# The first-layer gates of a two-layer hybrid mixer leave PSUM first, and the work behind its fixed first stage is placed anew

## The chip, the cores and the metric

The kernel runs on one core of one Trainium2 chip. The metric is device time in microseconds (us), the median of several executions; lower is better. A trace of one execution shows the engines: PE (TensorE, matmuls and transposes), DVE (VectorE), ACT (ScalarE), POOL (GpSimd) and SP, which here issues most of the DMAs. Each engine works through its own queue in order.

## What is computed

The reference is a trunk of two layers over 1024 tokens of width 1024. Cut to what matters:

```
for l in range(2):
  shift, scale, gate = split(SiLU(c) @ W_mod[l] + b_mod[l])
  h = RMSNorm(x) * (1 + scale) + shift
  aq,ak,av,ag, rq,rk,rv,rg, gq,gk,gv,gg,ga = split(h @ W_in[l])
  A = sliding_window_attention(rope(aq), rope(ak), av, sinks) * SiLU(ag)
  B = rms(retention(rot(rq), rot(rk), rv)) * SiLU(rg)
  C = rms(gated_linear_attention(gq, gk, gv, log_sigmoid(ga @ gw + gb) / 16)) * SiLU(gg)
  x = x + gate * RMSNorm(concat(A, B, C) @ W_out[l])
```

Everything is float32. The kernel makes each large product from three fp32r products, of high and low parts: hi x hi, lo x hi, hi x lo.

## The kernel before

**Tiles.** The tokens are eight tiles of 128. For each tile, `pre` (line 601) takes the norm: squares on ACT (L598), the sum and its power -0.5 (L582 on DVE, L583 on POOL), the scaling on DVE (L613). After a delay it transposes the tile on PE in two halves of four blocks (L620, printed under the helper's line L180), applies gain and shift (L627 on ACT for the first half, L629 on DVE for the second), and splits the result into its high part (L633, ACT) and low part (L634, DVE). The product of a tile with a weight unit of 256 columns is 24 matmuls (`accum`, printed under the helper's line L165).

**Gates.** Layer 0 begins with the gates, in four rounds of two tiles: unit `gg` (272 columns, with the low-rank logits) for both tiles, then `rg` (256) for both. Before the second half of the first x tiles is ready, `gg` of tiles 0 and 1 run over the first half alone. Each product lies in one of three PSUM banks (tag `mm`) until it has been taken out: for `gg`, L1084 copies the 16 logits and L1076 takes a tanh, both on ACT, and L1078 on DVE forms the SiLU; for `rg`, L1076 and L1078. The logits are transposed later and go through exponential and logarithm (L1106 to L1111). The SiLU values go to DRAM by SP. Behind the gates come `rq`, `rk` and `rv`, which need the sine and cosine tables (DVE L367 to L395, sine on ACT L391 and L392; L402 and four transposes per tile pair turn them round for later).

**What sets the order.** A hand-written first stage (`first`, line 660) issues the first modulation, x tiles 0 and 1, and the units `gg` and `rg`, inside a block in which DVE, ACT, POOL and SP keep the written order; the norms of tiles 2 and 3 are in that block too. PE keeps the written order everywhere. Outside the block a scheduler orders the other four engines ahead of time, by priority (written order, unless a block asks for high priority) among what it takes to be ready and to have a free tile. The written order comes from a planner: a clock `clk` that advances by a cost per PE instruction, and jobs (generators) that resume when the clock passes their due time. The due times are the table `L`. For the first layer's x tiles: `pf2` and `pf3` place the transposes of tiles 2 and 3; tile t of 4 to 7 takes its norm at `pf4 + pf5 * (t - 4)` and its transposes `pre1` = 7.44 later.

**Tiles in SBUF that matter.** `t2` (128x512) has ten buffers: x tiles 4 to 7 take eight (loaded by L639), and the normalised and modulated tiles need the same kind. `t1` has eight, `sm` eleven, and `st`, the staging tiles of weight loads, five. Weights come in four chunks per unit; `whi` (L758 on DVE or L760 on ACT) writes a chunk's high part, `wlo` (L763, POOL) its low part; later units do this in L149, L151 and L486.

**Small work.** POOL clears an accumulator for the gate part of the modulation (L309, whose first load is L310) and two large buffers of the linear attention (L877); these are held behind `mark[0]`, the power (L583) of tile 3. DVE halves `gnc` (L859) and copies the sinks (L888) from `sinkn`, an `sm` tile that SP fills.

Of the kernel before, what the change touches and what calls it, by code (L numbers as in the profile page):

```python
# [93 lines left out]
def trunk(ctx: ExitStack, tc: tile.TileContext, ins, cst, out):  # L94
    nc = tc.nc
    V, A, G, T = nc.vector, nc.scalar, nc.gpsimd, nc.tensor
# [4 lines left out]
    cp = ctx.enter_context(tc.tile_pool(name="const", bufs=1))  # L101
# [20 lines left out]
    def small(w, dt=F32):  # L122
        return gp.tile([P, w], dt, tag="sm", name=nm("sm"), bufs=BS)
# [7 lines left out]
    def f(ap):  # L131
        return ap.bitcast(F32)
# [11 lines left out]
    def eng(k):  # L144
        return G if EN[k] == "G" else V
# [251 lines left out]
    def tables_T():  # L397

        for p in range(NP_):
            yield L["tt1"]  # L400
            rep_ = t2()
            V.tensor_copy(rep_.rearrange("p (s t h k) -> p s t h k", s=2, t=2, h=4),  # L402
                          sincos[:, 2 * p:2 * p + 2, :, 0:32].rearrange("p t s k -> p s t k").unsqueeze(3)
                          .to_broadcast((P, 2, 2, 4, 32)))
            yield L["tt2"]
            pt = aux()
# [7 lines left out]
    gnc = cp.tile([P, DEPTH], F32, name="gnc")  # L414
# [126 lines left out]
    def sw_second():  # L541
        drain()
        for k in range(4):
# [46 lines left out]


    hT = {}
    mark = [None] * 2

    def squares(xt, to):
        ss = small(2)
# [4 lines left out]
    def pre(l, t, xt, soon=None):  # L601

        p, tt = divmod(t, 2)
        if tt == 0:
            hT[(l, p)] = place(TOK[l][p])
        h = hT[(l, p)]
        xn = [t2(), t2()]
        r = rstd2(squares(xt, xn))
        for j in range(2):
            if EN[f"xn{j}"] == "A":  # L610
                A.activation(xn[j], xt[j], AF.Copy, scale=r)
            else:
                V.tensor_scalar(xn[j], xt[j], r, None, ALU.mult)  # L613
        yield L[soon] if soon else lat("pre1", l)
        for j in range(2):
            yield (0.0, ("modh", l, j))
            x = aux()
            for k in range(4):
                kt = 4 * j + k
                transp(x[:, k * P:(k + 1) * P], xn[j][:, k * P:(k + 1) * P], ident)  # L620
            hf = t2()
            for k in range(4):
                kt = 4 * j + k
                ks = slice(k * P, (k + 1) * P)
                gain, shift = modc[(l, 1)][:, kt:kt + 1], modc[(l, 0)][:, kt:kt + 1]
                if EN[f"mod{j}"] == "A":
                    A.activation(hf[:, ks], x[:, ks], AF.Identity, scale=gain, bias=shift)  # L627
# [5 lines left out]
            A.activation(hi, hv, AF.Copy)  # L633
            eng(f"hlo{j}").tensor_tensor(lo, hv, f(hi), ALU.subtract)  # L634
        flag(("hT", l, t), 3.0)

    def load_x(t, xt, eng_):
# [22 lines left out]
    def first(wp):  # L660
# [54 lines left out]
        xn, at, ss, hv = {}, {}, {}, {}  # L715
# [39 lines left out]
        def whi(n, kc, st, e):  # L755
            d = w[n][:, 0, 2 * kc:2 * kc + 2, 0:256]
            if e is V:
                V.tensor_copy(d, st)  # L758
            else:
                A.activation(d, st, AF.Copy)  # L760

        def wlo(n, kc, st):
            G.tensor_tensor(w[n][:, 1, 2 * kc:2 * kc + 2, 0:256], st, f(w[n][:, 0, 2 * kc:2 * kc + 2, 0:256]),  # L763
                            ALU.subtract)
# [3 lines left out]
        sg = ga_load(0)  # L768
# [40 lines left out]
        rst = [next(rgen) for _ in range(4)]  # L809
# [7 lines left out]
        pc = cols_a(1)  # L817
        yield
        w["rg"] = unit(0, "rg")
        for kc in (0, 1):  # L820
            whi("rg", kc, rst[kc], A)
            wlo("rg", kc, rst[kc])
        cols_r(1, pc)
        for t in range(2):
# [34 lines left out]
    V.tensor_scalar(gnc, gnc, 0.5, None, ALU.mult)  # L859
    kv = {}  # L860

    gat = []
# [19 lines left out]
                gz["sc"] = [z_[:, 1024 * j:1024 * j + 1024].rearrange("p (c h q) -> p c h q", c=2, h=4)  # L882
                            for j in range(2)]
    sink8 = cp.tile([P, 2, 8], F32, name="sink8")
    sinkn = small(16)
    nc.sync.dma_start(sinkn, sinks.rearrange("(o a) b -> o (a b)", o=1).to_broadcast((P, 16)))
    for l in range(DEPTH):
        V.tensor_copy(sink8[:, l].rearrange("p (m r) -> p m r", r=2),  # L888
                      sinkn[:, 8 * l:8 * l + 8].rearrange("p (r m) -> p m r", r=2))
# [183 lines left out]
    def silu2(pg):  # L1073

        th = t1()
        A.activation(th, pg, AF.Tanh, scale=0.5)  # L1076
        sg = t1()
        V.scalar_tensor_tensor(sg, th, 1.0, pg, ALU.add, ALU.mult)  # L1078
        return sg


    def gla_logits(l, t, pg, pa):
        ga = small(16)
        A.activation(ga, pa, AF.Copy)  # L1084
# [683 lines left out]
L = {"sw1": 0.4, "ld1": 1.2, "ld2": 1.2, "ld1@1": 1.2, "ld2@1": 1.27, "swW00": 0.0, "swT1": 0.0, "swW11": 0.4, "swW10": 0.5, "tt1": 8.0, "tt2": 1.75, "tb1": 24.5, "tb2": 0.75, "pf2": 7.0, "pf3": 8.5, "pf4": 17.3, "pf5": 4.16, "mod1": 4.6, "mod2": 4.0, "mod3": 13.29, "mod4": 7.04, "mod5": 3.36, "mod6": 9.04, "pre1": 7.44, "kv1": 3.1, "kv2": 2.11, "aq1": 6.0, "aq7": 6.0, "ag1": 5.44, "aq2": 2.4, "aq6": 5.2, "aq3": 10.21, "aq4": 7.36, "aq5": 3.6, "hn1": 8.93, "hn2": 2.85, "gz1": 11.18, "gz2": 8.13, "gl1": 2.76, "gd3": 15.9, "gc1": 0.62, "gc2": 1.94, "gc3": 1.33, "gc4": 0.87, "gc6": 0.86, "gc5": 1.14, "rc1": 0.8, "rc2": 1.09, "rc3": 5.87, "rc4": 2.51, "fin1": 7.28, "lay1": 1.13, "gc4@1": 0.93, "mod2@1": 4.0, "mod3@1": 15.1, "mod5@1": 3.36, "mod6@1": 4.11, "pre1@1": 7.44, "kv1@1": 2.79, "kv2@1": 5.28, "aq1@1": 4.8, "aq7@1": 5.28, "ag1@1": 6.25, "aq2@1": 0.82, "aq6@1": 6.0, "aq3@1": 10.9, "aq4@1": 4.4, "aq5@1": 5.15, "hn1@1": 8.12, "hn2@1": 2.85, "gz1@1": 15.91, "gz2@1": 10.94, "gl1@1": 4.6, "gd3@1": 15.9, "gc1@1": 0.48, "gc2@1": 1.94, "gc3@1": 1.33, "gc6@1": 0.86, "gc5@1": 1.04, "rc1@1": 0.37, "rc2@1": 0.84, "rc3@1": 1.9, "rc4@1": 2.79, "fin1@1": 4.28, "lay1@1": 1.7}  # L1768
# [44 lines left out]
```

## Time and profile before

| what | us |
| --- | --- |
| median of 3 runs | 1010.38 |
| lowest and highest | 1010.09 and 1011.06 |
| the profiled execution | 1010.98 |
| its span, first to last instruction | 1009.3 |
| PE busy | 971.7 (96%) |
| DVE busy | 687.8 (68%) |
| ACT busy | 410.9 (41%) |
| POOL busy | 249.0 (25%) |
| mean granted PE clock | 0.985 |

How to read what follows: in a timeline, a line has its start in us from the span's start, its length, engine, source line (L1076 is line 1076 of the kernel before), operation, output and inputs by tile name, shape, and a count where equal instructions were merged; in brackets stands how long the engine was idle before it and who ended that. In the list of waits stand who waited for whom, the total, how often, and the longest. In a table of stretches stand for each stretch its length, the busy time of PE, PEld (weight loads), DVE, ACT and POOL with counts, then the granted PE clock, the share of the DMA engines and GB/s.

### The profile page before, as it was taken

To read this page: it belongs to the slowest core of one execution; us is meant where nothing else is said; L and a number is where in the kernel's file an instruction comes from. 1 tells how busy PE (TensorE), PEld (TensorE's weight loads), DVE (VectorE), ACT (ScalarE), POOL (GpSimd) and SP (SyncE) were. 2 spreads that over 40 slices of the span, in tenths; PEclk is the share of its full clock that TensorE was granted. 3 is DMA by queue.
4 is the path that set the end of the run, shared out by engine and by line. 5 is a ranking of instruction groups with operands and counts; after the bars stand their busy time and mean duration, and the time that the engine had idled before them with its cause. 6 is when DMAs were issued, how large, how long until landed. Compare 5 with 4: busy or idle time off the path is not lost.

```text
span 1009.3 us, 19637 instructions
## 1 busy us (share of the span) xinstructions
PE 971.7 (96%) x7133; PEld 828.2 (82%) x7133; DVE 687.8 (68%) x1673; ACT 410.9 (41%) x1154; POOL 249.0 (25%) x314
## 2 busy tenths in 40 slices
PE   6879899999999999999999999999999999999996
PEld 2579899988998777777889999997899877777775
DVE  4768856767766687664588285685676578567886
ACT  3457221333332556642356242123333266664331
POOL 2421101232421233430114010113232033544100
PEclk9888999999999999999999999999999999999999
DMA  9740611433325245668646151343132424378884
GB/s 330 274 149 22 194 47 58 144 118 112 116 85 178 82 143 155 207 178 267 210 154 214 48 158 55 96 141 106 43 116 86 125 76 135 112 233 261 266 262 139
DMA packets 112304, 148.76 MB, mean 147 GB/s; under 512 B 12064, under 2 KB 63820, under 8 KB 112208
## 3 DMA queue, kind: packets, MB, share of 16 engines
q1 hardware_dynamic: 106512, 137.96, 43.6%
q10 hardware_dynamic: 5696, 9.56, 2.6%
q8 instruction: 56, 0.92, 0.4%
q14 instruction: 40, 0.33, 0.1%
HBM read 109.20 MB, written 36.18 MB: 144 GB/s over the span
## 4 chain that ended last, share of the span: by engine, by line
PE 75%; DVE 8%; DMA 8%; issue 2%; ACT 2%; POOL 2%; SPq 0%; ACTq 0%; POOLq 0%; DVEq 0%
PE mm L165 57%; PE aux L165 14%; PE aux L180 4%; DMA st<-in_w_in_dram 3%; DVE arena L486 1%; DMA xk<-in_x_dram 1%; POOL sm L583 1%; DMA st<-in_w_last_dram 1%; DMA wm<-in_w_mod_dram 1%; DMA a<-mixS 1%; DVE t L613 0%; DVE st L547 0%; DVE t L1334 0%; DMA st<-in_w_mod_dram 0%; DVE t L1065 0%
## 5 line engine op out<-in xcount | busy, mean ns | idle before, releaser
L165 PE MATMUL mm<-arena,arena 128*128 128x256 f32 (+2 forms) x1824 | 301.6, 319 | 7.1 <-DVE t L1078 4.0
L165 PE MATMUL mm<-arena 128*128 128x256 f32 (+2 forms) x1824 | 300.8, 319 | 1.3 <-DVE t L1078 1.3
L165 PEld LDWEIGHTS mm<-arena,arena 128*128 128x128 f32 x1824 | 255.5, 191 | 32.1 <-issue 7.8
L165 PEld LDWEIGHTS mm<-arena 128*128 128x128 f32 x1824 | 256.2, 192 | 25.5 <-issue 3.3
L583 POOL TENSOR_TENSOR sm<-sm,mhalf 128x1 f32<-128x1 f32 (+1 forms) x64 | 55.4, 866 | 334.6 <-DVE sm L582 312.1
L165 PE MATMUL mm<-arena,mx 128*128 128x512 f32 (+1 forms) x564 | 130.5, 387 | 1.3 <-ACT kept L1427 1.3
L165 PEld LDWEIGHTS mm<-arena,mx 128*128 128x128 f32 x564 | 101.5, 188 | 25.2 <-ACT kept L1427 1.7
L149 ACT ACTIVATE t<-aux 128x256 f32<-128x256 f32 (+2 forms) x124 | 55.7, 467 | 75.1 <-PE aux L180 64.3
L149 ACT ACTIVATE arena<-st 128x512 fp32r<-128x512 f32 x94 | 56.2, 627 | 54.2 <-DMA st<-in_w_in_dram 19.9
L1015 POOL TENSOR_TENSOR smx<-smx,sm 128x512 f32<-128x512 f32 x32 | 35.7, 1116 | 128.2 <-DVE sm L1014 115.5
L486 DVE TENSOR_TENSOR arena<-st,arena 128x512 fp32r<-128x512 f32 x74 | 59.3, 826 | 4.2 <-ACT arena L149 1.5
L1011 ACT ACTIVATE smx<-smx,sm 128x129 f32<-128x129 f32 x128 | 49.9, 392 | 28.9 <-DVE sm L1008 28.8
L317 DVE SCALAR_TENSOR_TENSOR acc<-st,c_act,acc 128x512 f32<-128x512 f32 x60 | 47.5, 791 | 18.5 <-DMA st<-in_w_mod_dram 17.9
L486 POOL TENSOR_TENSOR arena<-st,arena 128x512 fp32r<-128x512 f32 x26 | 36.5, 1406 | 80.4 <-ACT arena L149 73.3
L180 PE MATMUL aux<-c_ident,t 128*128 128x128 f32 (+1 forms) x292 | 47.9, 281 | 5.0 <-DVE t L402 2.7
L180 PEld LDWEIGHTS aux<-c_ident,t 128*128 128x128 f32 (+1 forms) x292 | 34.9, 144 | 12.0 <-DVE t L402 2.9
L165 PEld LDWEIGHTS aux<-t,mx 32*128 32x128 f32 (+1 forms) x896 | 39.5, 187 | 3.9 <-issue 2.2
L1059 ACT ACTIVATE t<-aux 128x256 f32<-128x256 f32 x32 | 12.3, 383 | 73.2 <-PE aux L165 66.4
L165 PE MATMUL aux<-t,mx 32*128 32x32 f32 (+1 forms) x896 | 40.7, 272 | 0.0
L1006 DVE COPY_PREDICATED smx<-c_curmask,aux 128x256 f32<-128x256 int32 x64 | 25.4, 446 | 18.7 <-ACT smx L149 15.2
L627 ACT ACTIVATE t<-aux,mod,mod 128x128 f32<-128x128 f32 x56 | 21.5, 460 | 39.8 <-DVE t L1334 18.9
L1334 DVE SCALAR_TENSOR_TENSOR t<-t,sm,t 128x512 f32<-128x512 f32 x32 | 24.0, 780 | 18.7 <-DMA t<-in_x_dram 11.9
(230 smaller groups left out, 1406.2 us busy)
## 6 DMA issues: line engine op xcount, KB each, us to landing
st<-in_w_in_dram SPq DMA_DIRECT2D x96, 256.0 KB, 3.7
st<-in_w_mod_dram SPq DMA_DIRECT2D x64, 256.0 KB, 3.1
mx<-mixS SPq DMA_DIRECT2D x20, 512.0 KB, 5.5
mixS<-t SPq DMA_DIRECT2D x72, 128.0 KB, 3.4
st<-in_w_last_dram SPq DMA_DIRECT2D x36, 256.0 KB, 4.0
wm<-in_w_mod_dram SPq DMA_DIRECT2D x12, 512.0 KB, 6.8
t<-in_x_dram SPq DMA_DIRECT2D x24, 256.0 KB, 5.3
t<-tabS SPq DMA_DIRECT2D x16, 256.0 KB, 4.4
```

The lines of the kernel that those rows point to most:

```text
L149: A.activation(dst, src, AF.Copy)
L165: T.matmul(dst, lhsT, rhs, start=start, stop=stop)
L180: T.transpose(dst, src, idn)
L317: V.scalar_tensor_tensor(acc, wt, c_act[:, k:k + 1], acc, ALU.mult, ALU.add)
L486: e.tensor_tensor(lo, st, f(hi), ALU.subtract)
L583: mark[1] = G.tensor_tensor(r, r, mhalf[:, :w], ALU.pow)
L627: A.activation(hf[:, ks], x[:, ks], AF.Identity, scale=gain, bias=shift)
L1006: V.copy_predicated(sv, curmask.unsqueeze(1).to_broadcast((P, 2, P)), pv[:, :, n // P - 1, :])
L1011: A.activation(sm[:, h, :], sm[:, h, :], AF.Exp, bias=mx[:, h:h + 1], accum_out=sums[:, h:h + 1])
L1015: eng("pn").tensor_tensor(sm[:, :, 0:128], sm[:, :, 0:128], rs.unsqueeze(2).to_broadcast((P, 4, P)), ALU.mult)
L1059: A.activation(sq, po, AF.Square)
L1334: V.scalar_tensor_tensor(xt[j], yg[j], r, xt[j], ALU.mult, ALU.add)
```

## The change

- `silu2` (tanh and SiLU of both gates) and the copy of the logits are put in blocks of high priority.
- `mark[0]` becomes the power (L583) of tile 7 in place of that of tile 3, so the memsets L309 and L877 are queued on POOL behind it. `mark[2]` follows the latest L634.
- In `first`, all four chunks of `rg` are converted ahead of the second modulation of tiles 0 and 1 (chunk 2 on DVE, the others on ACT); before, chunks 2 and 3 were converted on DVE behind it.
- `pf2` and `pf3` grow by 1.0, `pf4` shrinks by 4.1.
- The halving of `gnc` and the copies of the sinks become a job due 44 us of the planner's time later, queued behind `mark[2]`; `sinkn` gets a buffer of its own.
- SBUF kept back for software DMA is set to 1024 bytes per partition.

```diff
-    mark = [None] * 2
+    mark = [None] * 3
...
                 V.tensor_scalar(xn[j], xt[j], r, None, ALU.mult)
+        if l == 0 and t == NT - 1:
+            mark[0] = mark[1]
         yield L[soon] if soon else lat("pre1", l)
...
-            eng(f"hlo{j}").tensor_tensor(lo, hv, f(hi), ALU.subtract)
+            mark[2] = eng(f"hlo{j}").tensor_tensor(lo, hv, f(hi), ALU.subtract)
...
-        for kc in (0, 1):
-            whi("rg", kc, rst[kc], A)
+        for kc in range(4):
+            whi("rg", kc, rst[kc], V if kc == 2 else A)
             wlo("rg", kc, rst[kc])
         cols_r(1, pc)
...
             flag(("hT", 0, t), 2.6)
-        for kc in (2, 3):
-            whi("rg", kc, rst[kc], V)
-            wlo("rg", kc, rst[kc])
         flag(("w", 0, "rg"), 3.0)
...
         pump()
-    mark[0] = mark[1]
     for t in range(4, NT):
...
-    V.tensor_scalar(gnc, gnc, 0.5, None, ALU.mult)
...
-    sinkn = small(16)
+    sinkn = cp.tile([P, 16], F32, name="sinkn")
     nc.sync.dma_start(sinkn, sinks.rearrange("(o a) b -> o (a b)", o=1).to_broadcast((P, 16)))
-    for l in range(DEPTH):
-        V.tensor_copy(sink8[:, l].rearrange("p (m r) -> p m r", r=2),
-                      sinkn[:, 8 * l:8 * l + 8].rearrange("p (r m) -> p m r", r=2))
+
+    def small_work():
+        yield 44.0
+        with tc.issue_after(mark[2].ins):
+            V.tensor_scalar(gnc, gnc, 0.5, None, ALU.mult)
+            for l in range(DEPTH):
+                V.tensor_copy(sink8[:, l].rearrange("p (m r) -> p m r", r=2),
+                              sinkn[:, 8 * l:8 * l + 8].rearrange("p (r m) -> p m r", r=2))
+
+    job(small_work())
...
         th = t1()
-        A.activation(th, pg, AF.Tanh, scale=0.5)
         sg = t1()
-        V.scalar_tensor_tensor(sg, th, 1.0, pg, ALU.add, ALU.mult)
+        with tc.high_priority():
+            A.activation(th, pg, AF.Tanh, scale=0.5)
+            V.scalar_tensor_tensor(sg, th, 1.0, pg, ALU.add, ALU.mult)
         return sg
...
         ga = small(16)
-        A.activation(ga, pa, AF.Copy)
+        with tc.high_priority():
+            A.activation(ga, pa, AF.Copy)
...
-L = {... "pf2": 7.0, "pf3": 8.5, "pf4": 17.3, "pf5": 4.16, ...}
+L = {... "pf2": 8.0, "pf3": 9.5, "pf4": 13.2, "pf5": 4.16, ...}
...
-    nc = _bacc.Bacc("TRN2", target_bir_lowering=False, num_devices=1)
+    nc = _bacc.Bacc("TRN2", target_bir_lowering=False, num_devices=1, dynamic_dma_scratch_size=1024)
```

More of the change, by code (lines that the diff above doesn't have):

```diff
@@ L1767 @@
 EN = {"shw0": "V", "shw1": "A", "shw2": "A", "shw3": "A", "slw0": "V", "slw1": "G", "slw2": "V", "slw3": "G", "sht2": "A", "sht3": "A", "sht4": "A", "slt2": "V", "slt3": "G", "slt4": "G", "sd": "V", "mh0": "A", "mh1": "A", "mh2": "A", "mh3": "A", "mf": "A", "ms0": "V", "ms1": "V", "ms2": "V", "ms3": "V", "yg0": "V", "yg1": "V", "ml0": "V", "ml1": "V", "ml2": "V", "ml3": "V", "mod0": "A", "mod1": "V", "qst": "S", "smh": "S", "sml": "S", "sm0": "S", "sm1": "S", "lao": "S", "sao": "S", "lmix": "S", "ssg": "S", "lsg": "S", "ssr": "S", "lsr": "S", "lx": "S", "sx": "A", "lw": "S", "lwm": "S", "whi0": "V", "whi1": "A", "whi2": "A", "whi3": "A", "wlo0": "V", "wlo1": "V", "wlo2": "V", "wlo3": "G", "xn0": "V", "xn1": "V", "hlo0": "V", "hlo1": "V", "rot0": "V", "rot1": "V", "rdec": "V", "kslo": "V", "qslo": "V", "vlo": "G", "kT": "A", "qT": "A", "sprev": "A", "pn": "G", "pf0": "A", "aoc": "A", "hng": "V", "mh": "A", "gso": "V", "mg": "V", "mgl": "V", "rT": "A", "rv": "A", "gv": "A", "gk": "A", "ak0": "V", "ak1": "V", "ak2": "V", "ak3": "V", "kd0": "G", "kd1": "G", "kd2": "G", "kx1": "G", "kx2": "G", "kx3": "V", "kx4": "V", "qb": "G", "stx": "V"}
-L = {"sw1": 0.4, "ld1": 1.2, "ld2": 1.2, "ld1@1": 1.2, "ld2@1": 1.27, "swW00": 0.0, "swT1": 0.0, "swW11": 0.4, "swW10": 0.5, "tt1": 8.0, "tt2": 1.75, "tb1": 24.5, "tb2": 0.75, "pf2": 7.0, "pf3": 8.5, "pf4": 17.3, "pf5": 4.16, "mod1": 4.6, "mod2": 4.0, "mod3": 13.29, "mod4": 7.04, "mod5": 3.36, "mod6": 9.04, "pre1": 7.44, "kv1": 3.1, "kv2": 2.11, "aq1": 6.0, "aq7": 6.0, "ag1": 5.44, "aq2": 2.4, "aq6": 5.2, "aq3": 10.21, "aq4": 7.36, "aq5": 3.6, "hn1": 8.93, "hn2": 2.85, "gz1": 11.18, "gz2": 8.13, "gl1": 2.76, "gd3": 15.9, "gc1": 0.62, "gc2": 1.94, "gc3": 1.33, "gc4": 0.87, "gc6": 0.86, "gc5": 1.14, "rc1": 0.8, "rc2": 1.09, "rc3": 5.87, "rc4": 2.51, "fin1": 7.28, "lay1": 1.13, "gc4@1": 0.93, "mod2@1": 4.0, "mod3@1": 15.1, "mod5@1": 3.36, "mod6@1": 4.11, "pre1@1": 7.44, "kv1@1": 2.79, "kv2@1": 5.28, "aq1@1": 4.8, "aq7@1": 5.28, "ag1@1": 6.25, "aq2@1": 0.82, "aq6@1": 6.0, "aq3@1": 10.9, "aq4@1": 4.4, "aq5@1": 5.15, "hn1@1": 8.12, "hn2@1": 2.85, "gz1@1": 15.91, "gz2@1": 10.94, "gl1@1": 4.6, "gd3@1": 15.9, "gc1@1": 0.48, "gc2@1": 1.94, "gc3@1": 1.33, "gc6@1": 0.86, "gc5@1": 1.04, "rc1@1": 0.37, "rc2@1": 0.84, "rc3@1": 1.9, "rc4@1": 2.79, "fin1@1": 4.28, "lay1@1": 1.7}
@@ new lines @@
+L = {"sw1": 0.4, "ld1": 1.2, "ld2": 1.2, "ld1@1": 1.2, "ld2@1": 1.27, "swW00": 0.0, "swT1": 0.0, "swW11": 0.4, "swW10": 0.5, "tt1": 8.0, "tt2": 1.75, "tb1": 24.5, "tb2": 0.75, "pf2": 8.0, "pf3": 9.5, "pf4": 13.2, "pf5": 4.16, "mod1": 4.6, "mod2": 4.0, "mod3": 13.29, "mod4": 7.04, "mod5": 3.36, "mod6": 9.04, "pre1": 7.44, "kv1": 3.1, "kv2": 2.11, "aq1": 6.0, "aq7": 6.0, "ag1": 5.44, "aq2": 2.4, "aq6": 5.2, "aq3": 10.21, "aq4": 7.36, "aq5": 3.6, "hn1": 8.93, "hn2": 2.85, "gz1": 11.18, "gz2": 8.13, "gl1": 2.76, "gd3": 15.9, "gc1": 0.62, "gc2": 1.94, "gc3": 1.33, "gc4": 0.87, "gc6": 0.86, "gc5": 1.14, "rc1": 0.8, "rc2": 1.09, "rc3": 5.87, "rc4": 2.51, "fin1": 7.28, "lay1": 1.13, "gc4@1": 0.93, "mod2@1": 4.0, "mod3@1": 15.1, "mod5@1": 3.36, "mod6@1": 4.11, "pre1@1": 7.44, "kv1@1": 2.79, "kv2@1": 5.28, "aq1@1": 4.8, "aq7@1": 5.28, "ag1@1": 6.25, "aq2@1": 0.82, "aq6@1": 6.0, "aq3@1": 10.9, "aq4@1": 4.4, "aq5@1": 5.15, "hn1@1": 8.12, "hn2@1": 2.85, "gz1@1": 15.91, "gz2@1": 10.94, "gl1@1": 4.6, "gd3@1": 15.9, "gc1@1": 0.48, "gc2@1": 1.94, "gc3@1": 1.33, "gc6@1": 0.86, "gc5@1": 1.04, "rc1@1": 0.37, "rc2@1": 0.84, "rc3@1": 1.9, "rc4@1": 2.79, "fin1@1": 4.28, "lay1@1": 1.7}
```

## The prediction

> **What bounds the kernel now.** I read the page first, then the waits of the matmul engine (PE), then the timeline of its first 130 us.
>
> ```profile
> span 1009.3 us, 19637 instructions
> PE   6879899999999999999999999999999999999996
> ```
> ```profile
> PE mm L165 <- DVE t L1078: 5.3, 2, 4.0
> PE mm L165 <- ACT arena L633: 3.2, 2, 2.2
> PE aux L180 <- DVE t L402: 2.7, 1, 2.7
> PE aux L180 <- DVE t L613: 1.8, 1, 1.8
> ```
>
> A digit is a tenth of a slice of 25 us. From the sixth slice to the last but one PE is at 9, so from about 125 us on its own work is the time; only the first five slices have room. The second view (total wait, times, longest) names the holes there: PE waits for the gate evacuation (L1078), for the normalised x tiles (L633, L613) and for the rotary tables (L402). Whatever closes such a hole ahead of 125 us should arrive at the end nearly in full, since PE runs back to back behind it. The span is 1009.3 us; the profiled execution took 1010.98, so 1.7 us lie around the span. My sum is made against 1010.98; the median of the three runs, 1010.38, is 0.6 below it.
>
> **First hole, 45 to 58 us.** PE's timeline there, then the other engines':
>
> ```profile
> 42.62 2.65 PE L165 MATMUL mm<-arena,arena 128*128 128x256 f32 x21
> 47.98 1.11 PE L180 MATMUL aux<-c_ident,t 128*128 128x128 f32 x8 [1.83 <-DVE t L613]
> 53.42 4.61 PE L165 MATMUL mm<-arena,arena 128*128 128x256 f32 x24 [3.97 <-DVE t L1078]
> 99.72 3.13 PE L165 MATMUL mm<-arena 128*128 128x256 f32 x24 [1.32 <-DVE t L1078]
> ```
> ```profile
> 48.69 1.50 ACT L627 ACTIVATE t<-aux,mod,mod 128x128 f32<-128x128 f32 x4 [6.98 <-PE aux L180]
> 52.31 0.18 ACT L1084 ACTIVATE sm<-mm 128x16 f32<-128x16 f32 x1
> 52.37 0.39 ACT L1076 ACTIVATE t<-mm 128x256 f32<-128x256 f32 x1
> ```
>
> The `mm` pool has three banks. The `gg` gates of tiles 0 and 1 and the `rg` gate of tile 0 fill them; the `rg` gate of tile 1 (53.42) needs the first bank back. Its product was complete before 42.62, when PE went on to `rg`. But ACT stands idle for 6.98 us with L627 of x tile 2 at its head and comes to L1084 and L1076 at 52.3, with DVE's L1078 behind them. As far as the trace shows, only their place in ACT's queue keeps them back: 3.97 us.
>
> The price goes on after the hole:
>
> ```profile
> 53.40:57.80 4.40, 4.38 (x24) 4.40 (x25) 3.52 (x12) 1.72 (x5) 1.57 (x3) 0.61 0.21 69
> 99.70:106.00 6.30, 6.28 (x52) 6.28 (x53) 6.19 (x15) 3.67 (x9) 2.43 (x5) 1.00 0.51 149
> ```
>
> In this table of stretches (length, then PE, PEld, DVE, ACT, POOL busy, granted clock) the 24 products behind the hole run at a clock of 0.61 and take 4.61 us; the same 24 at 99.72, at 1.00, take 3.13. So 1.5 us more belong to it. The Trainium skill, "TensorE: Matmul & The Clock Gate", part 1 on the clock gate, says that an idle window of about 3.4 us halves the clock until PE has been busy for as long. The trace agrees (0.61 behind 3.97 us); by that rule alone one half-clock window costs about 1.7 us, an estimate from the page.
>
> **Second hole, 70 to 81 us.**
>
> ```profile
> 61.10 0.18 ACT L1084 ACTIVATE sm<-mm 128x16 f32<-128x16 f32 x1 [2.58 <-PE mm L165]
> 61.44 0.64 ACT L598 ACTIVATE t<-t 128x512 f32<-128x512 f32 x1
> 63.82 0.88 DVE L613 TENSOR_SCALAR t<-t,sm 128x512 f32<-128x512 f32 x2 [0.66 <-POOL sm L583]
> 69.83 1.05 PE L180 MATMUL aux<-c_ident,t 128*128 128x128 f32 x8
> 73.20 0.76 PE L165 MATMUL mm<-arena,arena 128*128 128x272 f32 x4 [2.21 <-ACT arena L633]
> 77.55 3.81 PE L165 MATMUL mm<-arena,arena 128*128 128x272 f32 x17
> ```
>
> Tile 4 is transposed only when all gates of tiles 0 to 3 are through (69.83), and its modulation and split (L627 to L634) then lie bare: the 3.2 us of the waits, 2.21 of them at 73.20. The 17 products at 77.55 take 224 ns each, against 130 ns at 99.72: 1.6 us. Together 4.8.
>
> **The change part by part.**
>
> *Gates at high priority (L1076, L1078, L1084).* No operation is added. Banks come free at about 43 to 46 us, each evacuation taking 0.18 + 0.39 us of ACT. The 3.97 goes, and with it the 1.5 of slow clock: 5.5. In layer 1 the same priority gains nothing, since PE's digits are 9 there, in the middle of the span.
>
> *Memsets behind the norm of tile 7.* Rows of now:
>
> ```profile
> 43.59 0.88 DVE L613 TENSOR_SCALAR t<-mx,sm 128x512 f32<-128x512 f32 x2 [1.58 <-POOL sm L583]
> 45.47 2.85 DVE L613 TENSOR_SCALAR t<-mx,sm 128x512 f32<-128x512 f32 x2 [0.74 <-POOL sm L583]
> 45.84 1.80 POOL L877 MEMSET mx<- 128x2048 f32 x1
> 81.69 0.99 POOL L583 TENSOR_TENSOR sm<-sm,mhalf 128x1 f32<-128x1 f32 x1 [4.54 <-DVE sm L582]
> ```
>
> The same two L613 take 0.88 us alone and 2.85 beside the memset. Moved away, tile 3 is normalised 2.0 us earlier and the 1.83 before its transposes goes. The memsets (this one, its twin and the smaller one of `acc`) turn up past tile 7's norm, now at 81.69, where DVE is fuller. They cost it between 0 and the 2.0 us seen here; I charge the 2.0 below. SP's load of `acc` (L310) is queued behind the `acc` memset, and stores and weight loads behind that; nothing that PE needs at once, so 0, with 3 us as the far end, the length of the second hole.
>
> *The second half of `rg`'s conversion brought forward.*
>
> ```profile
> 33.11 1.13 ACT L760 ACTIVATE arena<-st 128x512 fp32r<-128x512 f32 x2
> 35.15 0.16 DVE L710 TENSOR_TENSOR sm<-mm,sm 128x4 f32<-128x4 f32 x1 [2.13 <-PE mm L165]
> 39.90 0.75 DVE L758 CAST arena<-st 128x512 fp32r<-128x512 f32 x2
> 40.40 2.65 POOL L763 TENSOR_TENSOR arena<-st,arena 128x512 fp32r<-128x512 f32 x2 [4.09 <-DVE arena L758]
> 36.44 0.81 ACT L743 ACTIVATE t<-aux,mod,mod 128x128 f32<-128x128 f32 x2 [2.20 <-DVE mod L712]
> ```
>
> One conversion more on ACT (0.57) ends at about 34.8, inside the 2.20 that ACT idles before 36.44; one on DVE (0.4) falls into the 2.13 that DVE waits for PE before L710. POOL then runs its two subtractions (2.65) right behind the first two instead of at 40.4 to 43, beside the modulation of tiles 0 and 1; taken as 0, and 1.9 at worst, what the memset cost L613. For that POOL is free at once for tile 2's L583, which stood behind them until 43.05.
>
> *Transposes (pf2 to pf5 and tile order).* Tiles 2 and 3 go 1 us later in PE's order: behind `rg` of tile 0, and seven products into `rg` of tile 1, which can now run. That is 0 where L613 is early. Tiles 4 to 7 go 4.1 us of the planner's time earlier, tile 4 into `rg` of tile 3, so that about 17 products (2.2 us) and the end of the first hole cover its modulation: of the 4.8 I count all, with 1.6 (clock alone) as the lower end. Their norms need free `t2` tiles (ten, of which the x loads take eight) from tiles 2 and 3, and these come some 2 to 3 us earlier.
>
> *Small work.*
>
> ```profile
> 53.84 0.16 DVE L859 TENSOR_SCALAR gnc<-gnc 128x2 f32<-128x2 f32 x1
> 54.23 0.23 DVE L888 COPY sink<-sm 128x8 f32<-128x8 f32 x2
> ```
>
> These leave the middle of tile 3's modulation and run later: some 0.4 us of DVE, moved and not saved. `sinkn` no longer takes one of eleven `sm` tiles. The DMA scratch setting moves addresses only; no software queue appears on the page (q1 and q10 are hardware). 0 for these.
>
> **What is late next: DVE.**
>
> ```profile
> 64.00:118.00 54.00, 46.81 (x363) 45.76 (x361) 45.17 (x111) 33.16 (x81) 8.99 (x16) 0.94 0.35 112
> 82.00:94.00 12.00, 12.00 (x101) 11.94 (x100) 10.92 (x26) 7.82 (x18) 1.64 (x5) 1.00 0.06 22
> 94.00:100.00 6.00, 4.68 (x37) 4.43 (x37) 4.33 (x10) 5.94 (x11) 0.43 (x2) 1.00 0.08 25
> 106.00:118.00 12.00, 9.31 (x81) 9.10 (x79) 10.57 (x30) 3.67 (x9) 1.36 (x1) 1.00 0.69 219
> 130.00:500.00 370.00, 368.12 (x2803) 312.73 (x2803) 248.10 (x625) 141.62 (x424) 92.16 (x113) 1.00 0.45 140
> ```
>
> The third busy number is DVE. The stall sum is 5.5 + 1.8 + 4.8 = 12.1 us. But from 64 to 118 us DVE has 45.2 us of work, 47.2 with the memsets' 2.0, and PE's last hole there (2.7 us, L402) is DVE's backlog. The stage up to 64 ends 7 us sooner (5.5 + 1.8, less 0.3 for tile 2's split), at 57. At the densest long stretch of now, 10.92 of 12 or 0.91, 47.2 us take 51.9 and end at 108.9: 9.1 us gained. At 0.88 (106 to 118) they take 53.6 and end at 110.6: 7.4. Some of that work (L317 for `modg`) can slip past 118 us. I take **8.5 us**: 1010.98 - 8.5 = 1002.5, and 0.6 lower for a median, **1002**.
>
> One more queue matters, ACT's function tables:
>
> ```profile
> 95.06 1.28 ACT L391 ACT_TABLE_LOAD   x1
> 96.35 0.64 ACT L391 ACTIVATE sincos<-t 128x512 f32<-128x512 f32 x1
> 99.24 0.42 DVE L1078 SCALAR_TENSOR_TENSOR t<-t,mm 128x256 f32<-128x256 f32 x1 [1.47 <-ACT t L1076]
> ```
>
> A gate's tanh put between logarithm and sine at high priority adds one load of 1.28 us, where ACT is nearly full (5.94 of 6 at 94 to 100). The 1.32 us before 99.72 therefore stays in my sum. The Trainium skill, "ScalarE: Activation LUTs", on what a table load costs, speaks against the change here: it adds 1.38 us of drain to each switch. The trace disagrees: the L391 load starts at 95.06 and its first sine at 96.35, 1.29 later. By the page one added switch would take about 2.7 us from the 8.5, an estimate.
>
> **The rivals.**
>
> *DVE takes it back.* The first hole goes, the second or the table stage keeps the rest: 3 to 7 us, 1004 to 1008, say 1005. For it: DVE at 0.88 before 118, the L402 wait. Against: from 130 us on DVE is busy 248.1 of 370 us, so a backlog drains there.
>
> *The gates still leave late.* L1084 and L1076 may be held by what they write (`sm`, `t1` tiles) and not by order. Then only the 1.8 for tile 3 and little else goes: 1009, or no change.
>
> *ACT blocks on gates (slower).* Place: ACT's queue, 57 to 90 us. A queue that meets a gate before PE has finished it waits, with the squares (L598) of the next x tile behind it; at 61.10 that costs 2.58 us today, ahead of L598. High priority can put every gate so. Price: 2.6 for each of tiles 4 to 7, 10.3 us on tiles that PE then awaits, against 5.5 gained early: about 5 slower, 1015. It decides as soon as such a wait exceeds the lead of the tile's transposes: by today's rows less 7 us, tile 4's squares come near 54.4 (61.44), its norm ends near 57.7 (63.82 + 0.88), and its transposes stand near 60.6 (69.83, and 2.2 for the 17 products), a lead of about 3. Against it: today's wait of 2.58 is under that lead.
>
> **How the numbers follow.** Forecast, 6.5 to 13.5 gained (997 to 1004): 0.55. DVE takes it back (1004 to 1008): 0.20. Gates late (1008 to 1011): 0.08, of which 0.05 is still faster. ACT blocks (1012 to 1018): 0.14. Better than all that (under 997; the L402 hole goes too): 0.03. The range 997 to 1010 holds the first three but for a sliver, 0.81. A measurement tells about 0.2% from no change: faster 0.55 + 0.20 + 0.05 + 0.03 = 0.83, same 0.03, slower 0.14.
>
> **What would show it.** Right: no PE wait on L1078 near 50 us, L1076 of the first gates before the first L627; L613 of tile 3 near 0.9 for two; clock 1.0 at 48 to 60; tile 4's transposes between products of `rg` tile 3; memsets L877 past the last L583 of the x tiles; the 24 products now at 99.72 (`rg` of tile 6) 8 to 12 us earlier, and the end 7 to 10. Wrong: ACT waits on PE at L1084 with L598 behind and PE waits on L633; a longer wait on L402; one more table load before the sine.

## The result, and the profile after

The changed kernel took 1006.28 us (median of 8 runs) against 1011.77 us for the kernel before: a ratio of 0.9935, 95% interval 0.9914 to 0.9956. One of the eight executions took 3279.62 us; the ratio leaves it out. A second series (`changed_again` below) gave 1003.52 against 1011.28, 0.9914 [0.9885, 0.9943]. The change is faster by 0.4 to 1.2%; by medians the gain is 5.5 and 7.8 us, against the 8.5 of the forecast. The forecast of 1002 lies 4.3 and 1.5 us below the two medians. Both lie in its range of 997 to 1010, but only the second lies in the 997 to 1004 of the forecast itself; 1006.28 lies in the 1004 to 1008 of the rival "DVE takes it back". The profiled execution took 1006.7 us, with a span of 1005.0.

The page of the changed kernel, span and PE's busy tenths (slices of 25 us), then its list of PE's waits (total, times, longest). In it the lines stand a little lower: L1090, L1082 and L1083 are the L1084, L1076 and L1078 of before, L635 is L633, L765 is L763, L753 is L751:

```profile
span 1005.0 us, 19647 instructions
PE   6989799999999999999999999999999999999896
```
```profile
PE aux L180 <- DVE posr L358: 6.0, 1, 6.0
PE aux L180 <- DVE t L402: 5.3, 1, 5.3
PE mm L165 <- DMA wm<-in_w_mod_dram: 3.7, 6, 1.3
PE mm L165 <- ACT arena L635: 3.4, 5, 1.6
```

The third digit went from 7 to 9, the fifth (100 to 125 us) from 8 to 7. The wait on the gates has gone from the list and the one on L402 has doubled, from 2.7 to 5.3. Then PE's timeline at the places that the prediction named:

```profile
45.65 3.00 PE L165 MATMUL mm<-arena,arena 128*128 128x256 f32 x24
...
49.28 1.07 PE L165 MATMUL mm<-arena,arena 128*128 128x256 f32 x7
...
50.98 2.25 PE L165 MATMUL mm<-arena,arena 128*128 128x256 f32 x17
...
54.29 3.31 PE L165 MATMUL mm<-arena 128*128 128x272 f32 x24 [0.47 <-ACT arena L635]
58.35 0.64 PE L165 MATMUL mm<-arena 128*128 128x272 f32 x3 [0.76 <-ACT arena L635]
...
70.36 1.16 PE L165 MATMUL mm<-arena,arena 128*128 128x272 f32 x7 [1.57 <-ACT arena L635]
...
71.39 2.37 PE L165 MATMUL mm<-arena,arena 128*128 128x272 f32 x17
...
92.17 5.92 PE L165 MATMUL mm<-arena 128*128 128x256 f32 x48
...
107.96 1.11 PE L180 MATMUL aux<-c_ident,t 128*128 128x128 f32 x4 [5.26 <-DVE t L402]
```

The wait on L402 in the kernel before was another one, for the second of these copies; the first came without a wait:

```profile
117.57 0.66 PE L180 MATMUL aux<-c_ident,t 128*128 128x128 f32 x4 [2.69 <-DVE t L402]
```

And the table of stretches, changed kernel (length, PE, PEld, DVE, ACT, POOL busy, clock):

```profile
47.00:61.00 14.00, 12.77 (x103) 12.27 (x103) 6.83 (x17) 8.19 (x22) 1.88 (x3) 1.00 0.29 85
61.00:109.00 48.00, 40.38 (x324) 39.20 (x324) 43.67 (x107) 33.90 (x79) 17.32 (x22) 0.99 0.40 125
```

Where the time came from is read off three pairs of rows. The `rg` products begin at 45.65 us; before, at 42.62. So this execution was 3.03 us behind at a place ahead of which, of the whole change, only the earlier conversion of `rg` could act. Most of that is no effect of the change: `changed_again`, the same kernel, is there at 43.42 (more on this in the last section). The products of `rg` of tile 6 begin at 92.17 against 99.72: 7.55 ahead, so 10.58 gained between the two places (10.66 in `changed_again`, 43.42 to 89.86). Then L402's wait gives back time: 5.26 against 2.69 before. That leaves 10.58 - 2.57 = 8.0. The spans differ by 4.3, or 7.3 with the 3.03 added, so 0.7 more is lost further back; I did not trace it.

### The profile page after: what moved, and what is told of

It is laid out like the page before. It is cut to its first block, busy times and chain, and to the rows that moved or that the text cites. A ratio compares the mean times of both kernels' runs of the same rounds, so it can differ in the third digit from the quotient of the medians.

```text
span 1005.0 us, 19647 instructions
## 1 busy us (share of the span) xinstructions
PE 968.2 (96%) x7133; PEld 825.1 (82%) x7133; DVE 683.4 (68%) x1672; ACT 413.8 (41%) x1156; POOL 252.9 (25%) x314
## 4 chain that ended last, share of the span: by engine, by line
PE 69%; DMA 11%; DVE 10%; ACT 4%; issue 3%; POOL 2%; SPq 1%; ACTq 0%; POOLq 0%; DVEq 0%
PE mm L165 52%; PE aux L165 13%; PE aux L180 4%; DMA st<-in_w_in_dram 2%; DMA wm<-in_w_mod_dram 1%; DMA st<-in_w_last_dram 1%; DMA t<-xs 1%; POOL sm L583 1%; DMA xk<-in_x_dram 1%; DMA out_dram<-t 1%; DVE t L1340 1%; DMA t<-in_x_dram 1%; DMA t<-aoS 1%; DVE arena L486 1%; SPq L154 1%
## 5 line engine op out<-in xcount | busy, mean ns | idle before, releaser
L583 POOL TENSOR_TENSOR sm<-sm,mhalf 128x1 f32<-128x1 f32 (+1 forms) x64 | 55.7, 870 | 316.9 <-DVE sm L582 294.8
L486 DVE TENSOR_TENSOR arena<-st,arena 128x512 fp32r<-128x512 f32 x74 | 57.1, 794 | 4.9 <-ACT arena L149 2.8
```

What stands on the lines that cost most here:

```text
L486: e.tensor_tensor(lo, st, f(hi), ALU.subtract)
L583: mark[1] = G.tensor_tensor(r, r, mhalf[:, :w], ALU.pow)
```

## Experiments

Times are medians beside runs of the kernel before on the same chip; ratios are to that kernel, with 95% intervals. The theories: **priority** (the prediction's: the gates left late because of their place in ACT's queue, and high priority moves them) against **tile order** (they left late because the `sm` tile that the logits' copy writes was handed out behind that of the sinks, whatever its priority).

### prio_only: high priority alone

```diff
         th = t1()
-        A.activation(th, pg, AF.Tanh, scale=0.5)
         sg = t1()
-        V.scalar_tensor_tensor(sg, th, 1.0, pg, ALU.add, ALU.mult)
+        with tc.high_priority():
+            A.activation(th, pg, AF.Tanh, scale=0.5)
+            V.scalar_tensor_tensor(sg, th, 1.0, pg, ALU.add, ALU.mult)
...
-        A.activation(ga, pa, AF.Copy)
+        with tc.high_priority():
+            A.activation(ga, pa, AF.Copy)
```

> The kernel before with nothing but the two blocks of high priority. If the gates left late because of their place in ACT's queue (the prediction): PE's wait on L1078's successor near 50 us goes, the clock stays full, 5.5 us faster, about 1005 us. If they were held by what they write (an sm or t1 tile), as the rival has it: PE still waits about 4 us for the first bank and the time is within 1 us of before.

Measured 1013.71 us, 1.0016 [0.9996, 1.0035]. PE's timeline and ACT's (L1086, L1078, L1079 are here the L1084, L1076, L1078 of before):

```profile
57.62 5.41 PE L165 MATMUL mm<-arena,arena 128*128 128x256 f32 x24 [3.97 <-DVE t L1079]
```
```profile
52.89 1.50 ACT L627 ACTIVATE t<-aux,mod,mod 128x128 f32<-128x128 f32 x4 [6.96 <-PE aux L180]
...
56.51 0.18 ACT L1086 ACTIVATE sm<-mm 128x16 f32<-128x16 f32 x1
56.58 0.39 ACT L1078 ACTIVATE t<-mm 128x256 f32<-128x256 f32 x1
```

The hole is the same to the hundredth, 3.97 us, and ACT still idles 6.96 us with tile 2's modulation at its head. The gates did not move in ACT's queue: L1086 starts 3.62 us behind the start of that L627, as L1084 does in the profile of before (48.69, 52.31). Priority alone gives no gain that the times show.

### sinkn_own: a buffer of its own for the sinks, alone

```diff
-    sinkn = small(16)
+    sinkn = cp.tile([P, 16], F32, name="sinkn")
...
-    nc = _bacc.Bacc("TRN2", target_bir_lowering=False, num_devices=1)
+    nc = _bacc.Bacc("TRN2", target_bir_lowering=False, num_devices=1, dynamic_dma_scratch_size=1024)
```

> The kernel before with sinkn in a buffer of its own (and the smaller DMA scratch that makes room), no priority, nothing moved. If the queue place is a matter of priority: no change. If the logits copy waited for an sm tile that sinkn stood ahead of: the first gates leave ahead of the modulation of tile 2, the wait of 4.0 us and the slow clock behind it go, 4 to 5.5 us faster, while the waits for tile 3 (1.8 us) and tile 4 (3.2 us) stay.

Measured 1003.65 us, 0.9917 [0.9895, 0.994]: the whole gain of the change from one line of its diff (and the DMA setting that makes room for it). Its ACT timeline, and PE's with all 16 transposes of tiles 2 and 3 in one row:

```profile
43.43 0.18 ACT L1084 ACTIVATE sm<-mm 128x16 f32<-128x16 f32 x1 [0.82 <-PE mm L165]
...
48.30 0.38 ACT L1076 ACTIVATE t<-mm 128x256 f32<-128x256 f32 x1 [4.41 <-PE mm L165]
48.58 1.50 ACT L627 ACTIVATE t<-aux,mod,mod 128x128 f32<-128x128 f32 x4
```
```profile
45.71 2.19 PE L180 MATMUL aux<-c_ident,t 128*128 128x128 f32 x16
47.66 3.44 PE L165 MATMUL mm<-arena,arena 128*128 128x256 f32 x27
```

The gates of tile 1 now leave at 43.43 (those of tile 0 at 42.18), ahead of L627, and PE has neither the 3.97 nor the 1.83 of waits. That is 8.7 us by medians, more than the 4 to 5.5 I had written down, since tile 3's wait, which I expected to stay, went as well; tile 4's stayed (2.58 us). Why the sinks? SP's queue of the kernel before, with the load of the sinks:

```profile
36.30 10.24 SPq L639 DMA_DIRECT2D t<-in_x_dram  x8
...
49.48 0.59 SPq L886 DMA_DIRECT2D sm<-in_attn_sinks_dram  x1
```

The eight x loads need 10 us there, 3.8 of them waiting for an L613 and 1.6 for transposes, and the sinks' load comes at 49.48. Its tile is asked for in the code ahead of those of the logits' copies (L1084), and these came at 52.31.

### no_prio: the change without high priority

```diff
-        with tc.high_priority():
-            A.activation(th, pg, AF.Tanh, scale=0.5)
-            V.scalar_tensor_tensor(sg, th, 1.0, pg, ALU.add, ALU.mult)
+        A.activation(th, pg, AF.Tanh, scale=0.5)
+        V.scalar_tensor_tensor(sg, th, 1.0, pg, ALU.add, ALU.mult)
...
-        with tc.high_priority():
-            A.activation(ga, pa, AF.Copy)
+        A.activation(ga, pa, AF.Copy)
```

> The changed kernel without the blocks of high priority. If priority carries the gain of the first hole: 5.5 us slower than the changed kernel, about as before. If it carries nothing there: within 1 us of the changed kernel (ratio to before 0.993), with no PE wait on the gates near 50 us.

Measured 1005.43 us, 0.9939 [0.992, 0.9958], against 0.9935 with it. The hole does not come back; waits on the SiLU of 0.2 to 0.6 us appear later. In its table of stretches PE is busy for all of 43 to 60 us, at full clock:

```profile
43.00:60.00 17.00, 17.00 (x140) 16.96 (x141) 10.59 (x29) 11.46 (x35) 3.49 (x10) 1.00 0.51 163
```

So the part that names the change is neither needed nor enough.

### more_sm and sinkn_first: number or order of the small tiles

`more_sm` gives the kernel before a twelfth `sm` buffer; `sinkn_first` leaves the sinks an `sm` tile, and asks for it and loads it ahead of the x loads.

```diff
-    B2, B1, BS, BST, MMB, SMB = 10, 8, 11, 5, 3, 3
+    B2, B1, BS, BST, MMB, SMB = 10, 8, 12, 5, 3, 3
...
-    nc = _bacc.Bacc("TRN2", target_bir_lowering=False, num_devices=1)
+    nc = _bacc.Bacc("TRN2", target_bir_lowering=False, num_devices=1, dynamic_dma_scratch_size=1024)
```

> The kernel before with one buffer more for the small tiles (BS 12 for 11) and nothing else of the change. Theory (the logits copy's tile is handed out behind the sinks' tile, because tiles of one tag go out in the order in which the code asks for them, so that another buffer doesn't help): the idle time of TensorE ahead of the rg products stays at about 4 us, on the first layer's SiLU, and the time is that of before within 2 us, a ratio of 0.998 to 1.002. Rival (there are only too few small tiles): that idle time goes as it does with the sinks in a buffer of their own, and the time is 5 to 9 us lower, near 1003 us, a ratio of 0.991 to 0.995.

```diff
+    sinkn = small(16)
+    nc.sync.dma_start(sinkn, sinks.rearrange("(o a) b -> o (a b)", o=1).to_broadcast((P, 16)))
     for t in range(4, NT):
         job(pre_first(t))
...
-    sinkn = small(16)
-    nc.sync.dma_start(sinkn, sinks.rearrange("(o a) b -> o (a b)", o=1).to_broadcast((P, 16)))
```

> The kernel before with the sinks' tile asked for, and its load issued, ahead of the x loads of the other tiles, the tile still one of the small tiles. Theory (the sinks' load stands behind x loads that wait for their tiles in SyncE's queue, and holds its small tile and all that are handed out behind it for as long): the 4 us of idle time ahead of the rg products go, and the time is 5 to 9 us lower than before, a ratio of 0.991 to 0.995. Rival (the sinks' buffer of its own is what counts, one small tile fewer in the ring for good): the wait stays at 3 to 4 us and the ratio is 0.998 to 1.002.

`more_sm` measured 1012.29 us, 1.0012 [0.9993, 1.0032]; `sinkn_first` 1007.65, 0.9966 [0.9952, 0.998]. PE's waits in `more_sm`, then SP's queue in `sinkn_first` (the sinks' load is L847 there), its DVE and PE:

```profile
PE mm L165 <- DVE t L1078: 4.6, 2, 3.4
```
```profile
38.54 0.33 SPq L847 DMA_DIRECT2D sm<-in_attn_sinks_dram  x1
```
```profile
46.24 2.80 DVE L613 TENSOR_SCALAR t<-mx,sm 128x512 f32<-128x512 f32 x2 [0.74 <-POOL sm L583]
```
```profile
49.09 0.66 PE L180 MATMUL aux<-c_ident,t 128*128 128x128 f32 x4 [0.88 <-DVE t L613]
49.50 3.44 PE L165 MATMUL mm<-arena,arena 128*128 128x256 f32 x27
54.00 4.20 PE L165 MATMUL mm<-arena 128*128 128x272 f32 x31 [1.05 <-ACT arena L633]
```

One more tile leaves 3.4 us of the hole; nor does the DMA setting, which is in `more_sm` too, bring anything by itself. The same tile loaded at 38.54 rather than 49.48 closes the hole: the 27 products run on from the transposes. With that, the number of tiles and the address are out; what fits all five runs is that tiles of one tag are handed out in the order in which the code asks for them, and that one whose load is late keeps back those behind it. How the scheduler arrives at this is argued, not shown, and `sinkn_first` moves the request and the load together. The gain, though, is 2.0 to 4.9 us by its interval, less than the 5 to 9 I wrote down. The rows show part of why: the memset again meets tile 3's L613 (2.80; in `sinkn_own`, where the memsets stand behind the same mark, the two took 1.11), and PE waits 0.88 and 1.05 us behind it. Counted from the start of `rg` to `rg` of tile 6 (44.25 to 94.63), 6.7 us are gained, against 7.9 in `sinkn_own` (43.23 to 92.39). The rest of the difference to `sinkn_own` I have not taken apart.

### old_pf: the change with the old due times

```diff
-"pf2": 8.0, "pf3": 9.5, "pf4": 13.2,
+"pf2": 7.0, "pf3": 8.5, "pf4": 17.3,
```

> The changed kernel with the old due times pf2 to pf4. By the prediction the second hole (3.2 us of PE waiting for tile 4's split, and its slow clock) comes back and the kernel is 3 to 5 us slower than the changed one up to 90 us. If that hole closes by itself once the first does, or the tables take the gain back: within 1 us of the changed kernel at the end.

Measured 1002.4 us, 0.99 [0.9865, 0.9935]. PE's waits, then the L402 row of its timeline:

```profile
PE mm L165 <- ACT arena L635: 6.8, 5, 2.2
```
```profile
97.67 1.01 PE L180 MATMUL aux<-c_ident,t 128*128 128x128 f32 x4 [2.21 <-DVE t L402]
```

The new due times do what they should at the x tiles: 3.4 us of waits instead of 6.8. From the start of `rg` to `rg` of tile 6 they are worth 3.0 us (46.52 us in the changed kernel, 49.49 here, 42.94 to 92.43). But L402 costs 5.3 instead of 2.2: with the old due times its first copy starts at 97.19, 0.6 us behind L395, and with the new ones 8.1 us behind. Together 8.7 against 9.0: gained early and given back later. At the end nothing is left that the two intervals can tell apart.

### tab_prio and rep_own: what holds L402

DVE is busy 43.67 of 48 us around L402, so a backlog was the first theory, and priority its remedy. The rival: L402's output `rep_` is a `t2` tile and waits for its turn, as the logits' copy did.

```diff
+            with tc.high_priority():
+                V.tensor_copy(rep_...)
```

> The changed kernel with the copies L402 (tables turned round) at high priority as well. If the 5.3 us that PE waits for L402 near 105 us are a matter of DVE's order: the wait goes, and with it the half-speed clock behind it, 5 to 7 us faster than the changed kernel, about 999 to 1001. If DVE's backlog as a whole is the bound: PE waits for the rotary of rq (L913) or the next banks instead and the gain is under 2 us.

```diff
-            rep_ = t2()
+            rep_ = gp.tile([P, 512], F32, tag="rep", name=nm("rep"), bufs=2)
```

> The changed kernel with the turned tables (L402) in a tag of their own, two buffers, in place of a t2 tile; no priority. If the copy waited for a free t2 tile: L402 comes right behind the cosine, PE's wait of 5.3 us near 105 us and the slow clock behind it go, 4 to 6 us faster than the changed kernel. If DVE's backlog is the bound (my forecast's reason): the wait turns up at the rotary or at the next banks, gain under 2 us.

`tab_prio`: 1002.91 us, 0.9914 [0.989, 0.9939], no better than `changed_again`. Neither outcome that I wrote down came: the wait stayed on the copy itself, 4.66 us (L403 there):

```profile
104.11 1.11 PE L180 MATMUL aux<-c_ident,t 128*128 128x128 f32 x4 [4.66 <-DVE t L403]
```

`rep_own`: 997.41 us, 0.9857 [0.9828, 0.9886], on the same chip as `changed_again`; all six executions (995.96 to 999.48) lie below all six of that run (1001.80 to 1005.25). DVE of the kernel before, of the changed one, then of `rep_own`, then a table of stretches of `rep_own`:

```profile
100.24 0.42 DVE L402 COPY t<-sincos 128x512 f32<-128x512 f32 x1
```
```profile
98.95 0.42 DVE L395 TENSOR_SCALAR sincos<-sincos 128x512 f32<-128x512 f32 x1
...
107.48 0.42 DVE L402 COPY t<-sincos 128x512 f32<-128x512 f32 x1
```
```profile
98.15 0.42 DVE L395 TENSOR_SCALAR sincos<-sincos 128x512 f32<-128x512 f32 x1
...
98.79 0.42 DVE L402 COPY rep<-sincos 128x512 f32<-128x512 f32 x1
```
```profile
61.00:109.00 48.00, 44.91 (x367) 43.75 (x366) 44.08 (x108) 34.41 (x81) 16.82 (x20) 1.00 0.36 118
```

The copy reads `sincos`, which L395 finishes; it runs 0.2 us behind L395 in `rep_own`, 8.1 us behind in the changed kernel, and 0.2 behind in the kernel before (L395 ends there at 100.00). DVE's work in the stretch is the same (44.08 and 43.67 us), and PE gets through 44.91 us of its own instead of 40.38. Of the wait, 0.95 us turn up at 107.40 on the rotary of `rq` (L916), the place that I had named for a backlog of DVE. So it was in the main the place of one copy of 0.42 us, not DVE's load. Which `t2` tile the copy stood behind I did not look up, and whether one more `t2` buffer would do as well was not run.

### sinkn_rep: two buffers and nothing else

The two buffers of `sinkn_own` and `rep_own` (with the DMA setting of the former), put into the kernel before.

```diff
-            rep_ = t2()
+            rep_ = gp.tile([P, 512], F32, tag="rep", name=nm("rep"), bufs=2)
...
-    sinkn = small(16)
+    sinkn = cp.tile([P, 16], F32, name="sinkn")
```

> The kernel before with sinkn in its own buffer and the turned tables in a tag of their own, nothing else. If free tiles set both holes: the first hole and the wait for L402 (2.7 us) go, 10 to 12 us faster than before, level with rep_own. If the other parts of the change (memsets, transposes, conversions) matter: 3 us or more behind rep_own.

Measured 1000.76 us, 0.9887 [0.9853, 0.9921], between `sinkn_own` and `rep_own`. The 3.3 us by which `rep_own` is ahead would be the other parts of the change, early transposes above all, now that nothing gives their gain back. The rows agree: from the start of `rg` to `rg` of tile 6 this kernel takes 49.81 us (43.67 to 93.48), `rep_own` 46.31 (45.06 to 91.37). But the intervals overlap and this is not settled.

### rep_oldrg and rep_oldmark: two parts taken back

Both stand on `rep_own`: one converts `rg` as before, the other holds the memsets behind tile 3 as before.

```diff
-        for kc in range(4):
-            whi("rg", kc, rst[kc], V if kc == 2 else A)
+        for kc in (0, 1):
+            whi("rg", kc, rst[kc], A)
             wlo("rg", kc, rst[kc])
...
+        for kc in (2, 3):
+            whi("rg", kc, rst[kc], V)
+            wlo("rg", kc, rst[kc])
```

> The changed kernel with the repeated sine and cosine tile in a buffer of its own (the run called rep_own, 997.4 us), and the conversion of the rg weights put back to where the kernel before has it. Theory (its place is worth nothing: the subtractions collide with GpSimd's when brought forward, but no product waits for them for more than 0.7 us): within 1.5 us of rep_own, 996 to 999 us. Rival (bringing it forward is what lets the rg products start behind the gates): a wait of 1 us or more on the converted rg weights near 45 us, and 2 to 4 us more than rep_own, 999 to 1002 us.

```diff
-        if l == 0 and t == NT - 1:
-            mark[0] = mark[1]
...
         pump()
+    mark[0] = mark[1]
     for t in range(4, NT):
```

> The changed kernel with the repeated sine and cosine tile in a buffer of its own (rep_own, 997.4 us), and the memset of the padded tiles put back to tile 3, where the kernel before has it. The prediction's step: the memset stretches a normalisation on VectorE from 0.88 to 2.85 us in the first stage and costs 1.8 us, so about 999.2 us. Rival (with the gates early, another normalisation or none is met, and tensor work stands ready beside it): within 1 us of rep_own, 996.5 to 998.5 us.

Measured 998.5 us, 0.9878 [0.9855, 0.9901], and 996.77 us, 0.9866 [0.9846, 0.9885], against 0.9857 for `rep_own`: neither part can be told from nothing, though intervals of this width, from another chip, could hide the 1.8 us that the prediction gave the memsets. DVE in `rep_oldmark`, and PE's wait there:

```profile
45.56 0.72 DVE L613 TENSOR_SCALAR t<-mx,sm 128x512 f32<-128x512 f32 x1 [0.74 <-POOL sm L583]
...
46.85 1.67 DVE L613 TENSOR_SCALAR t<-mx,sm 128x512 f32<-128x512 f32 x1
```
```profile
PE aux L180 <- DVE t L613: 0.2, 1, 0.2
```

The memset still stretches the second L613 (1.67 us; 0.48 in the changed kernel), but the transposes of tile 3 now stand seven products further back, and PE waits 0.2.

### changed_again

The changed kernel as it is, for a ratio from the same chip as `rep_own`, `sinkn_rep` and `old_pf`.

> The changed kernel once more, on the same chip as the next three, so that they are compared with it and not only with the kernel before. Expected ratio to before 0.993 to 0.994 (6 to 7 us), PE's wait on L402 again about 5 us, while the start of the gates moves by some us with the weights' arrival.

Measured 1003.52 us, 0.9914 [0.9885, 0.9943], with the L402 wait again (5.10). The best kernels of the study are `rep_own` and `rep_oldmark`, 14 and 15 us below the kernel before; `rep_own` is 6 below the changed one.

## Why the prediction came out as it did

The direction and the size were near; the cause of the largest term was wrong. The size is in part luck. The largest term was delivered by a line that the sum priced at 0, and the cut from 12.1 to 8.5 was made for a cause that did not act. Two of the three signs of being wrong that the prediction names also came: the longer wait on L402 and the table load more.

- **First hole, 5.5 us: right in size, wrong in cause.** The wait of 3.97 went, and the clock of 1.00 from 47 to 61 us (before, 0.61 behind the hole) brought the 24 products from 4.61 to about 3.3. The step that failed is the sentence "As far as the trace shows, only their place in ACT's queue keeps them back", and with it the credit to high priority: `prio_only` 1.0016, `no_prio` 0.9939. The line I priced at 0 ("`sinkn` no longer takes one of eleven `sm` tiles") did it: `sinkn_own` 0.9917. The rival "the gates still leave late" named the right hold, the `sm` tile the copy writes, but took it as untouched by the change. The clue was in the trace: an idle engine whose next operation has all its inputs, and a load of the same tag, 2.8 us ahead of it, at the end of a slow queue (49.48, 52.31).
- **Tile 3, 1.8 us: the wait went, but not through the memsets.** `sinkn_own` has them behind the same mark as before and no such wait: POOL, busy with the gates' logits, comes to L877 at 47.15 rather than 45.84, when the two L613 (46.03, 1.11 long) are done; `rep_oldmark` puts them back and PE waits only 0.2. Nor is the 1.83 a fixed price: the memset stretches tile 3's L613 by the same amount in `more_sm` and `prio_only` (2.85 each), and PE waits 2.69 for it in the one and 0.25 in the other, by where PE stood in that execution. At their new place the memsets (78.10 and 80.21) stretch tile 7's second L613 to 1.84, within the 2.0 that I charged; PE waits 0.15 for it.
- **Second hole, 4.8 us: about half.** The waits on the split were 3.2 and are 2.2 (3.4 less the 0.47 and 0.76 at tiles 2 and 3), and the 17 products take 2.37 instead of 3.81: 2.4 in all, inside my bounds of 1.6 and 4.8. Not all of that is due to the due times: in `old_pf` and `sinkn_own`, which have the old ones, the 17 products take 2.37 and 2.38 as well, while the waits on the split of tiles 4 to 7 are 5.1 in `old_pf`. The 0.47 and 0.76 at tiles 2 and 3 are new against before, and I had them at 0. They do not come from moving these tiles back, for `old_pf` has 0.55 and 1.18 there and `sinkn_own` 0.56: it fits that, with the first hole closed, PE is there sooner than the split.
- **Tables.** The 1.32 ahead of `rg` of tile 6, which I took as staying, went. One more table load did come before the sine, as I feared (and in `no_prio` too, so not by the priority): it lies at 92.58 on ACT, while PE runs without a wait from 92.17 to 102. ACT in the changed kernel:

```profile
92.58 1.28 ACT L1082 ACT_TABLE_LOAD   x1
93.88 0.39 ACT L1082 ACTIVATE t<-mm 128x256 f32<-128x256 f32 x1
94.28 1.28 ACT L391 ACT_TABLE_LOAD   x1
```

  The detour took 1.70 us of ACT from load to load. The Trainium skill, "ScalarE: Activation LUTs", on what a table load costs, counts 1.38 us of drain beside each load; the trace disagrees again, with the tanh 1.30 us behind the start of its load.
- **The cap by DVE: near in size, wrong reason.** I read the 2.7 on L402 as DVE's backlog and cut 12.1 to 8.5 because DVE has 0.88 to 0.91 of its time taken in this stage. Up to 92 us the stalls closed were worth 10.58, and 2.57 went back, so 8.0. But what took it back was not DVE's load: with `rep_` in its own buffer DVE does as much in the same stretch and PE waits 0.95 us there instead of 5.26. The 5.26 on L402 has the place and the sign of my rival "DVE takes it back", and another mechanism.
- **ACT blocks on gates** did not happen: ACT waits on PE at the gates, but what PE waits for the split of tiles 4 to 7 fell from 3.2 to 2.2 us.
- **Conversion of `rg`, small work, DMA setting.** Nothing measurable came of the first and the last, as priced (`rep_oldrg`, `more_sm`). In the rows the first is not free: its subtractions stretch L753, and in `rep_own` and `no_prio` PE waits 0.7 us for it, within the 1.9 I had at worst. The small work moved, 0.2 us each near 90, and was not tried by itself.

## What to carry to other kernels

When an engine idles while an operation whose inputs are ready stands further back, look first at what that operation writes: which tag, who was given a tile of that tag just ahead of it, and whether that one is stuck in a slow DMA queue. Where tiles go out in the order of the code, neither priority nor one more buffer need help; here a buffer or tag of its own for one tile did, twice (0.9917 for the late-loaded sinks, another 6 us for the repeated tables). And a change with six parts can owe all that one can measure to the line that looks like housekeeping: try the parts one by one before the name of the change is believed.

## What the runs showed of the hardware beside this

In these profiles POOL work stretches DVE's, the smallest too: in the changed kernel a DVE operation of 128x2, which took 0.17 us before, took 1.25 beside a POOL subtraction, and the two L753 of tiles 0 and 1 (0.69 each before) took 2.05 beside the `rg` subtractions brought forward:

```profile
100.19 1.25 DVE L1158 TENSOR_TENSOR gs<-gs,t 128x2 f32<-128x2 f32 x1
...
39.58 2.05 DVE L753 TENSOR_TENSOR arena<-t,arena 128x512 fp32r<-128x512 f32 x2
```
```profile
99.70 1.72 POOL L486 TENSOR_TENSOR arena<-st,arena 128x512 fp32r<-128x512 f32 x1 [3.30 <-ACT arena L149]
...
35.27 5.16 POOL L765 TENSOR_TENSOR arena<-st,arena 128x512 fp32r<-128x512 f32 x4 [8.10 <-DMA st<-in_w_in_dram]
```

The DVE operation of 128x2 ends at 101.44, the POOL subtraction beside it at 101.42. L588, of one column, shows the same: in the kernel before it takes 1.25 us beside POOL's subtractions (40.40 to 43.05), in the changed kernel, where these end at 40.43, 0.16:

```profile
40.57 1.25 DVE L588 TENSOR_TENSOR sm<-sm 128x1 f32<-128x1 f32 x1
...
42.17 0.16 DVE L588 TENSOR_TENSOR sm<-sm 128x1 f32<-128x1 f32 x1 [0.53 <-ACT t L598]
```

A slow clock on PE can follow an idle time shorter than the 3.97 us of the first hole. In the kernel before, the 24 products behind the 2.69 us on L402 took 4.55 us, at a granted clock of 0.57 (118 to 122 us), against 3.13 for 24 at full clock.

The first 40 us vary by themselves. The `rg` products begin at 42.62 in the profile of before, 45.65 in the changed one, 43.23 in `sinkn_own` and 48.42 in `prio_only`, though the edits of the last two touch nothing that runs ahead of there; part of it is the clock, 0.65 under the 48 products ahead of them in `prio_only`, which take 9.04 us, and 1.00 in `more_sm`, where they take 6.43. A single profile therefore carries several us that belong to no edit (42.42 in `more_sm` to 48.42), as much as most parts of this change, and gains were read from a place behind it:

```profile
39.55 9.04 PE L165 MATMUL mm<-arena 128*128 128x272 f32 x48
48.42 2.65 PE L165 MATMUL mm<-arena,arena 128*128 128x256 f32 x21
```
```profile
36.16 6.43 PE L165 MATMUL mm<-arena 128*128 128x272 f32 x48
```
